# Adding DMAs inside SBUF for two of four weight sums and for the inner blocks' sums to the residual, in a two-layer decoder trunk

## The chip, the core and the metric

The kernel runs on one NeuronCore of a Trainium2 chip. The metric is the device time of one execution in microseconds (us); three executions of the kernel before gave 1259.92, 1260.09 and 1260.38 us, so the median is 1260.09 us. PE is the matrix engine (PEld its weight loads), DVE the vector engine, ACT the scalar engine, POOL the GpSimd engine, SP the engine that issues most DMAs. PSUM is the memory that PE writes its sums to, SBUF the working memory.

## What is computed

A decoder trunk of two layers on 512 tokens with 1024 channels in float32. Each layer has a mixer (pooling, retention and sparse attention heads, one output projection), a layer norm, a gated feed-forward network (FFN) with a causal convolution of width 3, and a second layer norm. The change touches the FFN alone:

```python
def _conv_ffn(x, w_gate, w_up, conv_w, conv_b, w_down):   # x (512, 1024)
    hg = x @ w_gate                                       # (1024, 2816)
    hp = jnp.pad(hg, ((0, 0), (CONV_WIDTH - 1, 0), (0, 0)))
    hc = conv_b
    for kk in range(CONV_WIDTH):
        hc = hc + hp[:, kk:kk + t] * conv_w[kk]
    return (jax.nn.gelu(hc) * (x @ w_up)) @ w_down        # (2816, 1024)
...
x = _layernorm(DEEPNORM_ALPHA * x + f, ln2_g[l], ln2_b[l])
```

## The kernel before

**Precision.** Every product is made of three matmuls (`mm3`): each operand is split into a part that the matrix engine takes exactly (`hi`, a copy) and the rest (`lo`, a subtraction). A weight that was loaded as float32 into a `raw` tile therefore needs one copy, mostly on ACT, and one subtraction, on DVE or POOL, into a `w` tile before PE can use it.

**Tiling of the FFN.** The 2816 inner channels are 22 channel blocks of 128. The first three (`ff_plain`) are made directly. The other 19 of each layer (`ff_seven`) make gate and up of a channel block together by a scheme of seven instead of eight half-size products; it needs, per channel block, seven weight operands, of which three (`11`, `21`, `22`) are loaded and four (`t1` to `t4`) are sums of loaded ones. `load_seven` makes them: four DMAs of 256 KB fill the raw tiles `b` and `r`; one DVE addition of 128x1024 makes `t13` (`t1` and `t3`), two of 128x512 make the two halves of `t24`; seven `split` calls turn them into `w` tiles. `ff_seven` runs 84 matmuls of 256 columns on them; ACT copies its PSUM sums out several times in between, and PE accumulates further into the same PSUM bank after each copy.

**Down projection.** The 22 channel blocks are grouped as `BLOCKS` = 4, 3, 3, 3, 3, 6. When a group is done, 8 tiles (4 token tiles by 2 halves of 512 channels) of the down projection are made in PSUM from the group's `hT` tiles and added to the residual tiles `y` by `add_down`: DVE, 128x512, one operation each. They are mixed in among the matmuls of the next group's channel blocks.

**Order.** All instructions are recorded and then ordered by a list planner (`Plan.schedule`): it prices each (`price`), takes for each engine the first one that is ready by its model, and so writes one fixed order for each engine. At run time each engine works through its order and waits at an instruction whose inputs or buffer are not there yet; whatever stands behind it on that engine waits too. Buffers are pools of equal slots: 5 for `raw`, 14 for `w`, 29 for everything else of that size (`U`), 8 PSUM banks. An instruction that shares SBUF ports between DVE and POOL is kept from overlapping by the planner (`shares`).

Of the kernel before, what the change touches and what calls it, by code (L numbers as in the profile page):

```python
# [18 lines left out]
P = 128  # L19
# [133 lines left out]
class Plan:  # L153
# [49 lines left out]
    def shares(self, e, m, seen):  # L203

        if e == "vector":
            source = [v for read, v in seen if read and not v.tile.psum and int(np.prod(v.shape[1:])) > 1]
            return len(source) > 1 or (m in ("tensor_scalar", "tensor_copy") and not any(v.tile.psum for _, v in seen))
        return e == "gpsimd" and m != "memset"

    def price(self, op, seen):  # L210
        def size(v):
            return int(np.prod(v.shape[1:]))

        n = max([size(v) for _, v in seen] or [1])
        e, m = op.engine, op.method
        if e == "tensor":
            if m == "transpose":
                return 56 if op.args[2].shape[1] == 64 else 110
            n = size(op.args[2])
            return max(107, n * 0.4537)  # L220
        if e == "scalar":
            extra = sum(isinstance(op.kwargs.get(k), View) for k in ("bias", "scale")) + ("accum_out" in op.kwargs)
            return n * 0.833 + (52 if any(v.tile.psum for _, v in seen) else 95) + 92 * extra
        if e == "vector":
            if m == "reciprocal":
                return 6.3 * n + 70
            scalars = sum(isinstance(a, View) for a in (op.args[2:4] if m == "tensor_scalar" else op.args[2:3]))
            if m in ("tensor_scalar", "tensor_copy") and not any(v.tile.psum for _, v in seen):
                return 0.52 * n + 70 + 58 * scalars
            return 1.04 * n + 70 + 55 * scalars * (m == "scalar_tensor_tensor")  # L230
        if e == "gpsimd":
            if m == "memset":
                return n * 0.9 + 20
            if m == "tensor_copy":
                return n * 3.33 + 120
            if m == "tensor_scalar":
                return n * 1.24 + 120
            if op.args[-1] == OP.pow:
                return n * 165 + 300
            return n * 2.16 + 120  # L240
        byte = n * 4 * max(v.shape[0] for _, v in seen)
        return byte / 330.0

    def schedule(self):
# [35 lines left out]
        def opened(op):  # L280

            out = []
            for t in op.tiles:
                if t.got is None:
                    out.append(t)
                    if t.psum:
                        out += [f for f in t.follow if f.got is None and f not in out]
            return out
# [43 lines left out]
        while left:  # L332
            best = None
            for e in self.ENGINES:
                now = free[e]
                w, r = waiting[e], ready[e]
                while w and w[0][0] <= now:
                    heapq.heappush(r, heapq.heappop(w)[1:])
                cand = None
                skipped = []  # L340
                while r:
                    i = heapq.heappop(r)
                    skipped.append(i)
                    at = placed_at(ops[i[1]])
                    if at is not None and at <= now:
                        cand = (now, *i)
                        break
                    if len(skipped) > LOOK:
                        break
                if cand is None:  # L350

                    opts = []
                    for i in skipped:
                        at = placed_at(ops[i[1]])
                        if at is not None:
                            opts.append((at, *i))
                    for t0, *i in heapq.nsmallest(LOOK, w):
                        at = placed_at(ops[i[1]])
                        if at is not None:
                            opts.append((max(at, t0), *i))  # L360
                    if opts:
                        cand = min(opts)
                for i in skipped:
                    heapq.heappush(r, i)
                if cand is not None and (best is None or cand < best[:3]):
                    best = (*cand, e)
            assert best is not None, "no place for any instruction that is ready"
            start, _, i, e = best
            op = ops[i]
            if (op.rank, i) in ready[e]:  # L370
                ready[e].remove((op.rank, i))
                heapq.heapify(ready[e])
            else:
                waiting[e] = [x for x in waiting[e] if x[2] != i]
                heapq.heapify(waiting[e])
            op.start = start
            end = start + op.cost
            if e == "scalar" and op.method == "activation":
                f = op.args[2]
                if any(f in s for s in FUNCTIONS) and f not in functions:  # L380
                    functions = next(s for s in FUNCTIONS if f in s)
                    end += 1290
            if op.shared:
                held[e == "vector"] = end
            free[e] = end
            if e == "sync":
                free[e] = start + 60
                dma = max(getattr(self, "dma", 0.0), start + 600)
                self.dma = dma + op.cost
                end = self.dma + 1500  # L390
            elif e == "gpsimd":
                free[e] = end + 100
            op.opens = opened(op)
            op.wait = -1
            for t in op.opens:
                place = min(slots[t.key])
                slots[t.key].remove(place)
                t.got, t.after = place[0], place[2]
                if t.psum:
                    used[t.psum] += 1  # L400
            for t in op.tiles:
                t.last, t.by = max(t.last, end), e
                t.left -= 1
                if t.left == 0:
                    slots[t.key].append((t.last + 200, next(number), t))
                    if t.psum:
                        used[t.psum] -= 1
            for u in op.users:
                u.wait -= 1
                u.ready = max(u.ready, end + LATENCY[e][u.engine] * SLACK["wait"])  # L410
                if u.wait == 0:
                    heapq.heappush(waiting[u.engine], (u.ready, u.rank, u.index))
            done.append(op)
            left -= 1
# [12 lines left out]
def trunk(tc, x_d, pos_d, w_in, w_out, w_gate, w_up, w_down, cst_d, prm_d,  # L427
# [4 lines left out]
    with es:  # L432
# [84 lines left out]
        def load_seven(l, f):  # L517

            wg, wu = (w[l].rearrange("(h k p) c -> p h k c", p=P, h=2)[:, :, :, f * P:(f + 1) * P] for w in (w_gate, w_up))
            b, r = raw_tile(2, 4, P), raw_tile(2, 4, P)  # L520
            for out, src in ((b[:, 0], wg[:, 0]), (r[:, 0], wu[:, 0]), (b[:, 1], wu[:, 1]), (r[:, 1], wg[:, 1])):
                nc.sync.dma_start(out, src)
            t13, t24 = raw_tile(2, 4, P), raw_tile(2, 4, P)
            out = {}

            def split(name, src):
                w = w_tile(2, 4, P)
                nc.scalar.copy(w[:, 0], src)
                engine("v" if f >= NFF - 2 else SEVEN[name]).tensor_tensor(w[:, 1], src, w[:, 0].bitcast(F), OP.subtract)
                out[name] = (w[:, 0], w[:, 1])  # L530

            split("11", b[:, 0])
            nc.vector.tensor_tensor(t13, b, r[:, 0:1].to_broadcast([P, 2, 4, P]), OP.add)
            split("t1", t13[:, 0])
            split("21", r[:, 1])
            nc.vector.tensor_tensor(t24[:, 0], t13[:, 0], b[:, 1], OP.add)
            split("t2", t24[:, 0])
            split("22", b[:, 1])
            nc.vector.tensor_tensor(t24[:, 1], t24[:, 0], r[:, 1], OP.add)
            split("t3", t13[:, 1])  # L540
            split("t4", t24[:, 1])
            return out
# [335 lines left out]
        for l in range(L):  # L878
# [640 lines left out]
            def add_down(q, ib, t, lo, hi):  # L1519

                y = y_t[t][:, lo:hi]
                if ib == 0:
                    nc.vector.scalar_tensor_tensor(y, y, ALPHA, q, OP.mult, OP.subtract)
                else:
                    nc.vector.tensor_tensor(y, y, q, OP.subtract)

            xT2 = None
            wd = [None, None]
# [184 lines left out]
```

## Time and profile before

| | |
|---|---|
| median of 3 executions | 1260.09 us |
| profiled execution: its time, its span | 1259.87 us, 1258.1 us |
| granted TensorE clock, mean | 0.999 of 2.4 GHz |
| busy share PE, PEld | 98%, 89% |
| busy share DVE, ACT, POOL | 82%, 56%, 27% |
| chain of work that ended last: PE, DVE | 92%, 5% |
| DMA: mean rate, share of the 16 DMA engines in the load queue | 98 GB/s, 32% |

The span runs from the first to the last instruction; the profiled time has 1.8 us around it. Most operations are recorded through one helper, so that they all carry its line, L424; groups of the profile are told apart by their tiles. The busy time of PE overlaps from one matmul to the next, so that the pitch (start to start) is what a matmul costs, not its own duration.

### The profile page before, as it was taken

The numbers are of one execution on the slowest core, as the hardware profiler recorded it, in microseconds if no ns is written. First come the engines' busy times: TensorE is split into PE (matmuls) and PEld (weight loads), VectorE is DVE, ScalarE is ACT, GpSimd is POOL, SyncE is SP. The second block draws the span as 40 slices with busy tenths as digits, with TensorE's granted clock in tenths as the row PEclk, the third lists the DMA queues.
The fourth block names the chain that finished last, engine by engine and source line by source line (L and its number), as shares of the span: only waits on it lengthen the run. The fifth ranks groups of instructions, "written<-read, shape, count | busy, mean of one in ns | idle before, by whom it ended". The sixth has DMA issues, their size and how long they took to land.

```text
span 1258.1 us, 21371 instructions
## 1 busy us (share of the span) xinstructions
PE 1238.4 (98%) x8004; PEld 1120.6 (89%) x8004; DVE 1030.6 (82%) x1915; ACT 704.3 (56%) x1458; POOL 336.8 (27%) x247
## 2 busy tenths in 40 slices
PE   8999999999999999999999999999999999999997
PEld 6789898889998999999877898888899999999996
DVE  7868888788698988888877688888787889888876
ACT  6455578675545555556334455876764555555550
POOL 1133212352322322212111422133523222222023
PEclk9999999999999999999999999999999999999999
DMA  8321532102424333345253125221023333334221
GB/s 276 108 79 47 189 101 78 41 2 56 130 76 119 102 93 110 110 129 155 94 162 93 51 68 184 69 84 34 18 80 89 93 102 108 114 96 143 86 84 68
DMA packets 142600, 123.23 MB, mean 98 GB/s; under 512 B 6688, under 2 KB 116000, under 8 KB 142496
## 3 DMA queue, kind: packets, MB, share of 16 engines
q1 hardware_dynamic: 142496, 121.86, 32.0%
q8 instruction: 63, 1.03, 0.3%
q14 instruction: 41, 0.34, 0.1%
HBM read 117.65 MB, written 4.19 MB: 97 GB/s over the span
## 4 chain that ended last, share of the span: by engine, by line
PE 92%; DVE 5%; ACT 1%; issue 1%; SPq 0%; DMA 0%; POOL 0%; POOLq 0%; DVEq 0%; ACTq 0%
PE mm L424 46%; PE s L424 38%; PE tr L424 4%; PE pv L424 3%; DVE y L424 1%; DVE w L424 1%; DVE PT L424 1%; SPq L424 0%; DVE xq L424 0%; DMA raw<-in_w_up 0%; DVE VR L424 0%; DVE sm L424 0%; DVE rt L424 0%; ACT xq L424 0%; ACT xf L424 0%
## 5 line engine op out<-in xcount | busy, mean ns | idle before, releaser
L424 POOL TENSOR_TENSOR w<-raw,w 128x1024 fp32r<-128x1024 f32 (+3 forms) x116 | 234.2, 2020 | 636.4 <-ACT w L424 348.3
L424 ACT CAST w<-raw 128x512 fp32r<-128x512 f32 (+2 forms) x403 | 291.0, 742 | 196.8 <-PE s L424 117.9
L424 DVE TENSOR_TENSOR w<-raw,w 128x512 fp32r<-128x512 f32 (+3 forms) x288 | 236.0, 838 | 40.6 <-ACT w L424 36.1
L424 PE MATMUL mm<-w,hT 128*128 128x512 f32 (+1 forms) x1074 | 262.1, 391 | 1.7 <-ACT hT L424 1.7
L424 PE MATMUL s<-xq,w 128*128 128x256 f32 x1944 | 250.1, 281 | 0.1
L424 PEld LDWEIGHTS s<-xq,w 128*128 128x128 f32 x1944 | 242.4, 188 | 6.4 <-DVE sm L424 0.5
L424 PE MATMUL mm<-w,xT 128*128 128x512 f32 (+3 forms) x1152 | 240.7, 353 | 2.1 <-DVE w L424 1.8
L424 PE MATMUL s<-xs,w 128*128 128x256 f32 x1824 | 233.3, 280 | 0.0
L424 PEld LDWEIGHTS mm<-w,hT 128*128 128x128 f32 x1074 | 193.4, 188 | 39.5 <-ACT hT L424 1.9
L424 PEld LDWEIGHTS s<-xs,w 128*128 128x128 f32 x1824 | 225.3, 189 | 2.2
L424 PEld LDWEIGHTS mm<-w,xT 128*128 128x128 f32 x1152 | 191.0, 188 | 26.7 <-ACT xT L424 2.0
L424 DVE TENSOR_TENSOR raw<-raw,raw 128x512 f32<-128x512 f32 (+1 forms) x114 | 100.7, 883 | 6.0 <-DMA raw<-in_w_up 4.6
L424 DVE TENSOR_TENSOR y<-y,mm 128x512 f32<-128x512 f32 (+1 forms) x97 | 63.3, 674 | 19.8 <-PE mm L424 19.3
L424 ACT COPY pq<-s 128x256 f32<-128x256 f32 x152 | 55.1, 369 | 41.9 <-PE s L424 41.6
L424 PE MATMUL mm<-w,mixT 128*128 128x512 f32 x240 | 73.8, 414 | 0.0
L424 DVE SCALAR_TENSOR_TENSOR pq<-gu,prm,pq 128x511 f32<-128x511 f32 x76 | 67.1, 882 | 4.8 <-ACT pq L424 4.5
L424 POOL TENSOR_TENSOR sm<-sm,mhalf 128x1 f32<-128x1 f32 (+1 forms) x22 | 26.5, 1203 | 124.1 <-DVE sm L424 117.6
L424 DVE TENSOR_TENSOR gu<-s,pq 128x256 f32<-128x256 f32 x76 | 30.8, 419 | 27.7 <-PE s L424 23.7
L424 ACT ACTIVATE P<-s,sm 128x128 f32<-128x128 f32 (+3 forms) x96 | 49.4, 536 | 6.3 <-DVE sm L424 6.2
L424 DVE TENSOR_REDUCE sm<-s 128x1 f32<-128x384 f32 (+4 forms) x88 | 43.1, 528 | 8.6 <-PE s L424 7.9
L424 PEld LDWEIGHTS mm<-w,mixT 128*128 128x128 f32 x240 | 42.5, 189 | 7.0 <-ACT P L424 0.2
L424 PE MATMUL pv<-PT,VS 128*128 128x384 f32 x160 | 48.0, 364 | 0.7 <-ACT P L424 0.4
(203 smaller groups left out, 1654.8 us busy)
## 6 DMA issues: line engine op xcount, KB each, us to landing
raw<-in_w_gate SPq DMA_DIRECT2D x76, 256.0 KB, 3.4
raw<-in_w_up SPq DMA_DIRECT2D x76, 256.0 KB, 3.5
raw<-in_w_down SPq DMA_DIRECT2D x36, 512.0 KB, 3.9
raw<-in_w_in SPq DMA_DIRECT2D x32, 512.0 KB, 4.0
raw<-in_w_out SPq DMA_DIRECT2D x14, 512.0 KB, 3.8
raw<-in_w_in SPq DMA_DIRECT2D x8, 530.0 KB, 3.9
raw<-in_w_down SPq DMA_DIRECT2D x16, 256.0 KB, 2.8
raw<-in_w_in SPq DMA_DIRECT2D x8, 384.0 KB, 3.3
```

The source lines that it names most:

```text
L424: getattr(getattr(self.nc, op.engine), op.method)(*a, **k)
```

## The change

In `load_seven` the tile `r` is gone: the first half of `w_up` is loaded twice, straight into both halves of `t13`, and the fourth quarter of the weights straight into the second half of `t24`. The sum `t13 += b` (128x1024, 512 KB) is no longer a DVE addition but a DMA issued by POOL that adds into its target. In `add_down` the groups 1 to 4 no longer add on DVE: ACT copies the negated PSUM sum into a new `U` tile `yd`, and a DMA issued by POOL adds that tile (256 KB) to `y`. The first and the last group stay on DVE. The planner learns a price (900, times its slack of 1.2) and a latency (4500 ns) for such a DMA, and doesn't count it as sharing ports with DVE.

```diff
-        return e == "gpsimd" and m != "memset"
+        return e == "gpsimd" and m not in ("memset", "dma_start")
...
+            if m == "dma_start":
+                return 900
...
                 free[e] = end + 100
+                if op.method == "dma_start":
+                    end += 4500
...
-            b, r = raw_tile(2, 4, P), raw_tile(2, 4, P)
-            for out, src in ((b[:, 0], wg[:, 0]), (r[:, 0], wu[:, 0]), (b[:, 1], wu[:, 1]), (r[:, 1], wg[:, 1])):
+            b, t13, t24 = (raw_tile(2, 4, P) for _ in range(3))
+            for out, src in ((b[:, 0], wg[:, 0]), (t13[:, 0], wu[:, 0]), (b[:, 1], wu[:, 1]), (t13[:, 1], wu[:, 0]), (t24[:, 1], wg[:, 1])):
                 nc.sync.dma_start(out, src)
-            t13, t24 = raw_tile(2, 4, P), raw_tile(2, 4, P)
+            nc.gpsimd.dma_start(t13, b, accum_op=OP.add)
...
             split("11", b[:, 0])
-            nc.vector.tensor_tensor(t13, b, r[:, 0:1].to_broadcast([P, 2, 4, P]), OP.add)
             split("t1", t13[:, 0])
-            split("21", r[:, 1])
+            split("21", t24[:, 1])
...
-            nc.vector.tensor_tensor(t24[:, 1], t24[:, 0], r[:, 1], OP.add)
+            nc.vector.tensor_tensor(t24[:, 1], t24[:, 0], t24[:, 1], OP.add)
...
                     nc.vector.scalar_tensor_tensor(y, y, ALPHA, q, OP.mult, OP.subtract)
+                elif ib == len(BLOCKS) - 1:
+                    nc.vector.tensor_tensor(y, y, q, OP.subtract)
                 else:
-                    nc.vector.tensor_tensor(y, y, q, OP.subtract)
+                    tmp = U([P, 512], n="yd")
+                    nc.scalar.activation(tmp, q, AF.Copy, scale=-1.0)
+                    nc.gpsimd.dma_start(y, tmp, accum_op=OP.add)
```

## Rows read from the trace of the kernel before

**Rows 1.** The page, part 1: busy time, share and instructions of each engine.
```profile
PE 1238.4 (98%) x8004; PEld 1120.6 (89%) x8004; DVE 1030.6 (82%) x1915; ACT 704.3 (56%) x1458; POOL 336.8 (27%) x247
```

**Rows 2.** Busy time by stretch: the FFN of layer 0 (three), of layer 1 (three).
```profile
core 0: us, PE busy (x) PEld busy (x) DVE busy (x) ACT busy (x) POOL busy (x), PEclk, DMA share, GB/s
290.00:400.00 110.00, 107.48 (x790) 101.58 (x790) 89.61 (x122) 60.63 (x110) 27.50 (x15) 1.00 0.33 94
400.00:600.00 200.00, 200.00 (x1425) 187.62 (x1424) 172.75 (x250) 116.30 (x218) 47.39 (x26) 1.00 0.40 117
600.00:660.00 60.00, 59.56 (x278) 48.22 (x277) 49.97 (x96) 17.70 (x32) 11.18 (x7) 1.00 0.40 125
913.00:1030.00 117.00, 116.22 (x856) 110.10 (x855) 97.53 (x136) 66.38 (x120) 29.60 (x16) 1.00 0.32 95
1030.00:1200.00 170.00, 170.00 (x1209) 159.35 (x1209) 147.69 (x214) 96.26 (x185) 37.85 (x22) 1.00 0.36 106
1200.00:1250.00 50.00, 49.87 (x295) 43.81 (x293) 36.45 (x60) 16.16 (x27) 16.55 (x12) 1.00 0.21 74
```

**Rows 3.** Busy PE, 400 to 600 us, tile s alone, then tile mm alone.
```profile
400.00:600.00 200.00, 140.70 (x1142) 1.00 0.40 117
...
400.00:600.00 200.00, 71.47 (x283) 1.00 0.40 117
```

**Rows 4.** Chain that ended last, 400 to 480 us: start, duration, what.
```profile
442.30 7.12 PE s L424 x60
...
454.15 2.32 PE mm L424 x10
```

**Rows 5.** Groups of instructions (busy, mean ns | idle before); DVE, then ACT.
```profile
L424 DVE TENSOR_TENSOR y<-y,mm 128x512 f32<-128x512 f32 x95 | 62.4, 679 | 17.8 <-PE mm L424 17.4
...
L424 DVE TENSOR_TENSOR raw<-raw,raw 128x1024 f32<-128x1024 f32 x38 | 48.8, 1284 | 4.6 <-DMA raw<-in_w_up 4.6
...
L424 ACT COPY xf<-tr 128x512 f32<-128x512 f32 x16 | 9.6, 601 | 0.0
```

**Rows 6.** Groups, 400 to 600 us: the same two of DVE, POOL's longest.
```profile
L424 POOL TENSOR_TENSOR w<-raw,w 128x1024 fp32r<-128x1024 f32 x9 | 23.4, 2599 | 77.0 <-ACT w L424 37.2 <-PE s L424 32.0 <-ACT gu L424 7.7
L424 DVE TENSOR_TENSOR y<-y,mm 128x512 f32<-128x512 f32 x32 | 20.8, 679 | 2.4 <-PE mm L424 2.2
...
L424 DVE TENSOR_TENSOR raw<-raw,raw 128x1024 f32<-128x1024 f32 x12 | 15.8, 1316 | 0.9 <-DMA raw<-in_w_up 0.9
```

**Rows 7.** Timeline (start, duration in us): one channel block's load, sum, cast, use.
```profile
430.35 0.37 SPq L424 DMA_DIRECT2D raw<-in_w_gate  x1
...
437.98 1.21 DVE L424 TENSOR_TENSOR raw<-raw,raw 128x1024 f32<-128x1024 f32 x1
...
445.21 0.62 ACT L424 CAST w<-raw 128x512 fp32r<-128x512 f32 x1 [1.06 <-PE s L424]
...
457.72 1.58 PE L424 MATMUL s<-xs,w 128*128 128x256 f32 x12
```

**Rows 8.** Timeline: the cast of the next channel block's first sum.
```profile
455.79 1.15 ACT L424 CAST w<-raw 128x512 fp32r<-128x512 f32 x2 [0.38 <-DVE raw L424]
```

**Rows 9.** Timeline, 388 to 397 us: DVE waits for a load, PE idles.
```profile
392.26 1.23 DVE L424 TENSOR_TENSOR raw<-raw,raw 128x1024 f32<-128x1024 f32 x1 [2.89 <-DMA raw<-in_w_up]
...
395.88 1.44 PE L424 MATMUL mm<-w,hT 128*128 128x512 f32 x5 [1.72 <-ACT hT L424]
```

**Rows 10.** Waits of DVE over the span: total, times, longest.
```profile
DVE raw L424 <- DMA raw<-in_w_up: 4.6, 3, 2.9
```

**Rows 11.** DMA, 400 to 600 us; then issues of the span: KB, us to landing.
```profile
DMA packets 29848, 23.39 MB, mean 117 GB/s; under 512 B 1120, under 2 KB 24672, under 8 KB 29830
...
raw<-in_w_down SPq DMA_DIRECT2D x12, 512.0 KB, 4.0
...
xs<-y SPq DMA_DIRECT2D x4, 512.0 KB, 2.9
...
y<-xs SPq DMA_DIRECT2D x4, 512.0 KB, 7.2
```

## The prediction

> **What bounds the kernel now.** I read the engines' shares first: PE is busy for 98% of the span, DVE for 82%, ACT for 56%, POOL for 27% [rows 1]. A busy PE need not be a full one, so I went on to the FFN by stretches [rows 2]. In the middle of each layer's FFN, 400 to 600 us and 1030 to 1200 us, PE is busy for 200.00 of 200 and 170.00 of 170 us, at a granted clock of 1.00. The pitch tells whether that is real work. The chain shows 60 matmuls of 256 columns in 7.12 us, 0.1187 us each, and 10 of 512 columns in 2.32 us, 0.232 us each [rows 4]. In 400 to 600 us there are 1142 of the first and 283 of the second kind [rows 3]: 1142 x 0.1187 + 283 x 0.232 = 135.6 + 65.7 = 201 us, for 200 us of time. PE runs matmul after matmul at its own pitch there, and nothing that DVE does is waited for. DVE is busy for 172.75 of these 200 us, ACT for 116.30, POOL for 47.39 [rows 2]: DVE is close to full and still isn't the bound.
>
> What PE loses in the FFN is the rest of these stretches: 2.52 us in the first, 0.44 in the third, 0.78 in the fourth and 0.13 in the last, 3.9 us in all [rows 2]. One piece of it I can follow: DVE waited 2.89 us for a load before a sum of weights, what stood behind that sum came late, and PE idled for 1.72 us [rows 9]. Everything outside these stretches belongs to mixer, norms and the end, which the change doesn't touch.
>
> **What goes.** 38 sums of 128x1024 leave DVE, 48.8 us together [rows 5], and 4 groups x 8 tiles x 2 layers = 64 additions to the residual at 679 ns, 43.5 us [rows 5]. In 400 to 600 us that is 15.8 + 20.8 = 36.6 us [rows 6], so DVE falls from 172.75 to 136 us of 200. On the path this is worth 0, because PE is full there without it. The cover needs no work to hide it: the removed work was itself hidden. At most it gives back the 3.9 us of PE's losses.
>
> **What comes on ACT.** 64 copies of a 128x512 PSUM tile. The nearest row is ACT's copy of such a tile at 601 ns [rows 5]: 64 x 0.6 = 38.5 us, 19 us of them in 400 to 600 us, so ACT rises from 116 to 136 us of 200. That stays under PE's 200 and costs 0 as a sum. It stands, though, on the engine whose copies PE waits for within a channel block; one of these copies can be late by the 0.6 us that another takes. From PE's side a wait of 2.89 us cost 1.72 us, and the other two of the three DMA waits, 4.6 - 2.9 = 1.7 us together, cost nothing that shows [rows 9, 10]. So I take 0 for a delay of 0.6 us, with 64 x 0.6 = 38 us as an end that would need every copy on the path.
>
> **What comes on POOL.** 102 DMA issues. The trace has no DMA issued by POOL. The nearest rows are SP's issue at 0.37 us [rows 7] and POOL's own longest operation in the stretch at 2.6 us [rows 6]; between them 38 to 265 us on an engine that is idle for about three quarters of the FFN. In 400 to 600 us there are 12 + 32 = 44 issues: at 1 us POOL goes from 47 to 91 us, at 2.6 us to 162 of 200. It costs 0 in either case as a sum. Behind a waiting issue stand POOL's subtractions for `21` and for the down weights, and behind these SP's loads, which need their raw slots.
>
> **What comes on the DMA engines.** Each channel block loads `wu`'s first half once more (256 KB), adds 512 KB inside SBUF, and the residual 64 times 256 KB. In 400 to 600 us that is 12 x 0.26 = 3.1 MB of loads and 12 x 0.52 + 32 x 0.26 = 14.7 MB of additions on top of 23.39 MB, which took a share of 0.40 [rows 2, 11]. If a byte that is added costs what a loaded one does, the share becomes 0.40 x 41.2/23.4 = 0.70; if it costs double, because the target is read too, 0.40 x 55.9/23.4 = 0.96. I take a value between, some 0.8: the added rows are 2 and 4 KB long, and most packets of the loads are under 2 KB [rows 11].
>
> **Where the new waits stand.** The trace has no adding DMA, so its latency is bounded: a transfer of 512 KB out of SBUF lands in 2.9 us, the slowest group of 512 KB transfers into it in 7.2 us [rows 11]. The planner reckons 0.9 x 1.2 + 4.5 = 5.6 us. I take 5.6 us, near the middle, and let 3 to 9 us be the ends. Now the slack. In the row of one channel block the load was issued at 430.35, the sum ran at 437.98, the cast of `t1` at 445.21, after waiting for PE to free a `w` slot, and PE used it at 457.72 [rows 7]. From sum to cast there are 7 us, from cast to use 12.5 us. The next block has less: its cast waited 0.38 us for the sum [rows 8]. But the change needs three raw slots per channel block where there were four (`b`, `r`, `t13`, `t24`), so of five slots two, not one, are free for the next block's `b` and `t13`, and the adding DMA can start before the previous block's casts are done, up to one block's PE time (84 x 0.1187 = 10 us) earlier. That hides 5.6 us, and mostly 9 us. The additions to `y` are needed one group later, some 40 us; only their `yd` slot is held. The term is 0, with an end of 38 x 1.72 = 65 us if each adding DMA cost PE what the one late load did [rows 9].
>
> **Sum.** 1259.87 (profiled; the median is 0.2 us above) - 0 to 3.9 + 0 = 1256 to 1260; I take **1260.0 us**, since the one traceable loss hangs on a load, and loads get more company.
>
> **The rivals.**
>
> **The weight sums come late** (slower). An ACT cast or DVE sum behind an adding DMA waits at the head of its engine, and PE's PSUM copies stand behind it. This decides from a latency beyond what the planner reckoned plus about 1 to 3 us: three DMA waits show that 1.7 us in two cost nothing and 2.9 us cost 1.72 us [rows 9, 10]. With a quarter of 38 sums so late: 9.5 x 1.72 = 16 us, 1276 us. With all: 1325 us. For it speak the load bursts that such a DMA shares the engines with and the fixed order; against it the 7 + 12.5 us of slack [rows 7]. The Trainium skill has a rule that would bring this about: "SBUF — State Buffer", summary of rules for kernel authors, says that a DMA issued by GpSimd is starved of descriptor writing while DVE runs in its two-port fast modes. The stretch's large DVE groups that I read are two-operand additions [rows 6], which that page does not count among these modes, so I give the rule no more than a part of this chance.
>
> **DVE's relief reaches PE** (faster). All 3.9 us of PE's losses go: 1259.9 - 3.9 = 1256.0 us. For it: the one loss that I can follow runs through DVE [rows 9]. Against: its cause was a load, not DVE's work, and the rest is fractions of a microsecond.
>
> **The DMA engines become the bound** (much slower). If an added byte costs three times a loaded one, the share in 400 to 600 us is 0.40 x 70.6/23.4 = 1.2, and the FFN's 707 us [rows 2] grow by up to 20%, 140 us; at a share of 1.05 by 35 us, 1295 us. The Trainium skill, "DMA: Bandwidth & Descriptors", section on issuing engines not being separate DMA queues, says that DMAs of SP, ACT and GpSimd share the same 16 engines; no run here shows it for GpSimd yet.
>
> That the change doesn't do what it says, in that the work still falls on DVE, is ruled out by the edit; that it buys nothing is my forecast.
>
> **How the numbers follow.** Forecast (within the FFN's slack) 0.53; sums late 0.27; DMA engines the bound 0.08; relief reaches PE 0.12. What a measurement here can tell from no change is about 0.2%, 2.5 us. The likeliest case alone is 1257.5 to 1262.5 us. The range of 8 in 10 takes in the relief (1256) and the first half of the late sums (1276). Faster 0.12, same 0.53, slower 0.35.
>
> **What would show it.** In the profile after: DVE's busy time down by about 92 us, ACT's up by about 38 us, PE still at 200 of 200 in the middle of the FFN, no wait for the adding DMA over 2 us on ACT or DVE, DMA share in the FFN's middle about 0.7 to 0.95. I am wrong if PE idles before a matmul that waits for an ACT copy behind a wait for `t13` or a `yd` slot, or if loads land several us later than now.

## The result and the profile after

The changed kernel took 1280.26 us (median of four executions, 1279.74 to 1280.77) against 1260.10 us before it: ratio 1.0155, 95% interval 1.0143 to 1.0167. It is 20 us slower, outside the range of 1256 to 1276 us. The profiled execution has a span of 1278.0 us, 19.9 us more than before.

The page of the changed kernel, part 1 and the DMA queues of part 3 (packets, MB, share of 16 engines); these lines answer to [rows 1]:

```profile
PE 1246.0 (97%) x8004; PEld 1124.6 (88%) x8004; DVE 963.8 (75%) x1813; ACT 736.8 (58%) x1522; POOL 419.9 (33%) x349
...
q1 hardware_dynamic: 162560, 131.83, 34.0%
q0 software_dynamic: 14688, 36.71, 16.4%
```

The work moved as intended: DVE lost 66.8 us of busy time, ACT gained 32.5 us, POOL 83.1 us. The cost appears at PE: span less busy time was 19.7 us and is 32.0 us, so 12.3 of the 19.9 us are PE's idle time. Of the other 7.6 us some 3.8 us are the clock: the mean granted clock fell from 0.999 to 0.996, 0.004 x 1278 - 0.001 x 1258 = 3.8 us, an estimate from rounded means. The last 3.8 us lie in gaps too short to show between overlapping matmuls, or elsewhere; I could not assign them.

Busy time by stretch of the changed kernel, columns as in [rows 2]:

```profile
290.00:400.00 110.00, 109.74 (x810) 104.25 (x811) 82.88 (x117) 64.61 (x114) 33.93 (x23) 1.00 0.55 141
400.00:500.00 100.00, 98.43 (x682) 90.90 (x681) 70.49 (x101) 62.80 (x124) 45.43 (x38) 1.00 0.84 195
500.00:600.00 100.00, 93.53 (x675) 87.83 (x674) 66.48 (x99) 58.05 (x112) 26.86 (x24) 0.98 0.79 193
...
1030.00:1130.00 100.00, 99.80 (x699) 92.66 (x699) 73.46 (x98) 63.00 (x122) 43.94 (x38) 1.00 0.84 195
1130.00:1200.00 70.00, 65.01 (x462) 60.98 (x460) 47.51 (x69) 42.28 (x84) 25.21 (x22) 0.98 0.84 194
1200.00:1250.00 50.00, 48.05 (x311) 43.39 (x312) 31.64 (x45) 25.07 (x45) 11.58 (x8) 1.00 0.45 114
```

Start at PE's column. The first stretch is better than before, 109.74 of 110 us instead of 107.48 [rows 2]. The next loses 1.6 us. Only the last group of channel blocks is bad: 6.5 us are lost in 500 to 600 us, 5.0 us in 1130 to 1200 us and 2.0 us in 1200 to 1250 us. The DMA share, 0.32 to 0.40 before over the same stretches up to 1200 us [rows 2], is 0.55 in the first stretch and 0.79 to 0.84 from 400 to 600 and from 1030 to 1200 us.

The waits of the changed kernel (total, times, longest) name the path; before, only the first line has a counterpart, DVE's 4.6 us for a load [rows 10]:

```profile
DVE raw L428 <- DMA raw<-raw: 45.7, 18, 6.2
ACT w L428 <- DMA raw<-raw: 34.0, 18, 4.1
PE s L428 <- ACT pq L428: 13.6, 10, 3.2
ACT hT L428 <- DMA y<-yd: 2.6, 2, 1.9
```

DVE and ACT wait 36 times for the adding DMAs of the weight sums (`raw<-raw`), and PE waits for ACT's copies of PSUM sums (`pq`), which need no DMA. How the one becomes the other is seen in one place, in the timeline of the changed kernel (start, duration, what, idle before and its releaser):

```profile
520.53 1.73 SPq L428 DMA_DIRECT2D raw<-in_w_up  x2
...
528.13 0.88 POOL L428 DMA_DIRECT2D raw<-raw  x1 [5.07 <-DMA raw<-in_w_up]
...
535.43 1.66 ACT L428 CAST w<-raw 128x512 fp32r<-128x512 f32 x3 [3.38 <-DMA raw<-raw]
535.43 0.69 DVE L428 TENSOR_TENSOR raw<-raw,raw 128x512 f32<-128x512 f32 x1 [5.71 <-DMA raw<-raw]
...
538.22 0.63 ACT L428 COPY pq<-s 128x256 f32<-128x256 f32 x2
...
538.63 4.61 PE L428 MATMUL s<-xs,w 128*128 128x256 f32 x24 [2.53 <-ACT pq L428]
```

The load is issued at 520.5, and POOL can issue the sum only at 528.1, when the last of the loads is there. The sum lands 7.3 us later. ACT and DVE have stood at the head of their queues for 3.4 and 5.7 us; ACT must now make three casts, an activation and a fourth cast before it reaches the copy that PE wants, and PE idles for 2.5 us. The clock follows, in stretches of 10 us of PE alone (PE busy, granted clock, DMA share, GB/s):

```profile
530.00:540.00 10.00, 7.47 (x59) 0.99 0.57 122
540.00:550.00 10.00, 10.00 (x60) 0.84 0.52 145
```

After the stretch in which PE was busy for 7.47 us of 10, the granted clock of the next is 0.84, a mean of the levels 2.4 and 1.2 GHz; 10 x 0.16 = 1.6 us more are gone.

### The profile page after: what moved, and what is told of

Its sections match the earlier page's. It is cut to its first block, busy times and chain, and to the rows that moved or that the text cites. A ratio compares the mean times of both kernels' runs of the same rounds, so it can differ in the third digit from the quotient of the medians.

```text
span 1278.0 us, 21809 instructions
## 1 busy us (share of the span) xinstructions
PE 1246.0 (97%) x8004; PEld 1124.6 (88%) x8004; DVE 963.8 (75%) x1813; ACT 736.8 (58%) x1522; POOL 419.9 (33%) x349
## 3 DMA queue, kind: packets, MB, share of 16 engines
q1 hardware_dynamic: 162560, 131.83, 34.0%
q0 software_dynamic: 14688, 36.71, 16.4%
## 4 chain that ended last, share of the span: by engine, by line
PE 80%; DMA 8%; DVE 6%; issue 3%; ACT 2%; POOL 1%; SPq 1%; POOLq 0%; ACTq 0%; DVEq 0%
PE mm L428 42%; PE s L428 30%; PE tr L428 5%; PE pv L428 3%; DMA raw<-raw 3%; DMA raw<-in_w_up 2%; DVE w L428 2%; DMA raw<-in_w_gate 1%; DMA y<-yd 1%; DVE y L428 1%; ACT w L428 1%; DVE PT L428 1%; SPq L428 1%; DVE raw L428 0%; POOL y L428 0%
## 5 line engine op out<-in xcount | busy, mean ns | idle before, releaser
L428 PE MATMUL s<-xs,w 128*128 128x256 f32 x1824 | 237.2, 284 | 14.8 <-ACT pq L428 13.2
L428 DVE SCALAR_TENSOR_TENSOR pq<-gu,prm,pq 128x511 f32<-128x511 f32 x76 | 61.4, 808 | 34.1 <-ACT pq L428 33.3
L428 POOL DMA_DIRECT2D y<-yd x64 | 58.0, 925 | 85.9 <-ACT yd L428 73.7
L428 DVE TENSOR_TENSOR raw<-raw,raw 128x512 f32<-128x512 f32 x38 | 30.6, 805 | 45.8 <-DMA raw<-raw 45.7
L428 DVE TENSOR_TENSOR hT<-pq,hT 128x512 fp32r<-128x512 f32 x38 | 50.6, 1332 | 18.6 <-ACT hT L428 18.5
L428 POOL TENSOR_TENSOR sm<-sm,mhalf 128x1 f32<-128x1 f32 (+1 forms) x22 | 27.5, 1250 | 107.7 <-DVE sm L428 101.2
L428 POOL DMA_DIRECT2D raw<-raw x38 | 34.4, 905 | 74.5 <-DMA raw<-in_w_up 38.7
L428 POOL TENSOR_SCALAR P<-P,sm 128x384 f32<-128x384 f32 (+3 forms) x40 | 22.2, 569 | 86.2 <-DVE sm L428 72.8
```

The costliest lines, as they stand in the source:

```text
L428: getattr(getattr(self.nc, op.engine), op.method)(*a, **k)
```

## The experiments

Every run stands beside the kernel before on the same chip (1260.3 to 1261.7 us); ratios are to it.

**One half of the change at a time.** `weights_only` keeps the diff in `load_seven` and puts `add_down` back:

```diff
-                elif ib == len(BLOCKS) - 1:
-                    nc.vector.tensor_tensor(y, y, q, OP.subtract)
                 else:
-                    tmp = U([P, 512], n="yd")
-                    nc.scalar.activation(tmp, q, AF.Copy, scale=-1.0)
-                    nc.gpsimd.dma_start(y, tmp, accum_op=OP.add)
+                    nc.vector.tensor_tensor(y, y, q, OP.subtract)
```

> Only the weight sums are made by adding DMAs (38 of 512 KB, and the first half of w_up loaded twice); all sums to the residual stay on DVE. Changed kernel 1280.3 us, before 1260.1 us. Theory 'late weight sums' (ACT and DVE stand at the head of their queues for the 512 KB adding DMA, which lands later than the 5.6 us that the order reckons): the cause is all here, 1272 to 1281 us. Theory 'crowded DMA engines' (share 0.82 in the FFN's middle, so that loads and adding DMAs are late together): a third to a half of the slowdown is left, 1264 to 1270 us, and the adding DMAs land 1 us or more earlier than the 5.9 us median. Theory 'held yd slots and ACT's extra copies': 1260 to 1262 us.

Measured: 1259.11 us, ratio 0.9986 (0.9977 to 0.9996). `residual_only` keeps the diff in `add_down` and puts `load_seven` back.

> Only the inner groups' sums to the residual are made by adding DMAs (64 of 256 KB, each after a copy on ACT); the weight sums are as before the change. 'Late weight sums': 1259 to 1262 us. 'Crowded DMA engines': 1262 to 1268 us. 'Held yd slots and ACT's extra copies': 1272 to 1281 us.

Measured: 1266.88 us, ratio 1.0047 (1.0032 to 1.0062). The halves cost -1.9 and +5.9 us, the whole +20: some 16 us arise only from the two together. None of the three theories fits both runs: the one that lets the weight sums alone cost nothing puts the whole slowdown on the sums to the residual. The waits for the weight sums in `weights_only`:

```profile
ACT w L428 <- DMA raw<-raw: 13.7, 12, 3.1
DVE raw L428 <- DMA raw<-raw: 12.8, 12, 2.8
PE s L428 <- ACT pq L428: 0.4, 1, 0.4
```

24 waits of up to 3.1 us, 26.5 us in all, cost PE 0.4 us. Waits of that size are covered; those of the changed kernel, up to 6.2 us, are not.

**Another reckoned latency.** `plan_8us`:

```diff
-                    end += 4500
+                    end += 8000
```

> The changed kernel, but the planner reckons 8000 ns instead of 4500 ns for an adding DMA, so that what needs its result is put later in the order; the work is the same. 'Late weight sums': what stood behind the wait now stands ahead of it; most of the slowdown goes, 1261 to 1268 us. 'Crowded DMA engines': the DMAs stay as slow and PE still runs out of weights, 1275 to 1285 us.

Measured: 1267.14 us, ratio 1.0050 (1.0033 to 1.0067). The same work in another order gives two thirds of the slowdown back, as the late sums want it. The waits that were 45.7 and 34.0 us, in this run:

```profile
ACT w L428 <- DMA raw<-raw: 5.5, 2, 3.8
DVE raw L428 <- DMA raw<-raw: 4.7, 3, 2.2
```

**Half as many bytes to add.** `half_weight_add`:

```diff
-            nc.gpsimd.dma_start(t13, b, accum_op=OP.add)
+            nc.gpsimd.dma_start(t13[:, :, 0:2], b[:, :, 0:2], accum_op=OP.add)
```

> The changed kernel in the same order on every engine, but each adding DMA of the weight sums adds only half of its elements (256 instead of 512 KB); the other half of the two sums is left out of the computation. 'Late weight sums': the DMA lands 1 to 2 us earlier, inside what the order reckons, and most of the slowdown goes: 1261 to 1268 us. 'The order itself is worse' (ACT's extra copies, the slots): 1277 to 1281 us. 'Crowded DMA engines': in between, 1268 to 1274 us.

Measured: 1281.89 us, ratio 1.0163 (1.0145 to 1.0180). This speaks against the late sums. Its queue and issues:

```profile
q0 software_dynamic: 19552, 26.75, 12.8%
...
L428 POOL DMA_DIRECT2D raw<-raw x38 | 47.1, 1240 | 64.5 <-DMA raw<-in_w_up 32.0
```

With 10 MB less there are 19552 instead of 14688 packets, because each row is now two pieces of 1 KB instead of one of 4 KB; POOL's issue takes 1240 ns instead of 905. The run changed two things at once and decides nothing about the bytes. It leaves an open end: its weight sums land in 4.8 us in the median instead of 5.9, and ACT and DVE wait 18.4 and 30.0 us for them instead of 34.0 and 45.7, yet PE's waits for `pq` grew from 13.6 to 17.1 us. What made up for the earlier landing (POOL's issues grew) was not tested. The next three runs shorten the DMAs without more pieces.

**Duration taken away in the unchanged order.** Only at the point where the planned instructions are issued, each adding DMA is cut to one short piece of each row (64 KB in all); every engine's order stays that of the changed kernel, and the rest of the sums is left out. The edit of `tiny_both`; `tiny_residual` and `tiny_weights` keep one of the cases:

```diff
+            if op.engine == "gpsimd" and op.method == "dma_start":
+                weights = len(op.args[0].shape) == 4
+                if weights:
+                    a = [v[:, 0, 0] for v in a]
+                if not weights:
+                    a = [v[:, 0:128] for v in a]
```

> The changed kernel in its own order on every engine, all 102 adding DMAs kept, but each adds only 128 elements of a row (64 KB instead of 512 and 256 KB); the rest of these sums is left out. Theory 'adding DMAs land late and crowd the loads': with almost nothing to move they land in 2 to 3 us and the time falls to 1258 to 1263 us. Theory 'the written order and POOL's queue' (ACT's copies stand ahead of weight casts, issues wait behind issues): stays at 1272 to 1281 us.

> The same, but only the 64 sums to the residual are cut to 64 KB; the weight sums add their full 512 KB. 'Late through crowding, both streams': 1262 to 1270 us. 'Late weight sums alone': 1272 to 1280 us. 'Order and POOL's queue': 1272 to 1281 us.

> The same, but only the 38 weight sums are cut to 64 KB; the sums to the residual add their full 256 KB. 'Late through crowding, both streams': 1262 to 1270 us. 'Late weight sums alone': 1258 to 1264 us, and then the run with halved weight sums stayed slow only because its halves, two pieces in a row, doubled the descriptors. 'Order and POOL's queue': 1272 to 1281 us.

| weight sums | sums to the residual | time, us | ratio to before |
|---|---|---|---|
| 512 KB | 256 KB | 1280.3 | 1.0155 (1.0143 to 1.0167) |
| 512 KB | 64 KB | 1265.9 | 1.0046 (1.0031 to 1.0061) |
| 64 KB | 256 KB | 1257.7 | 0.9978 (0.9969 to 0.9988) |
| 64 KB | 64 KB | 1257.7 | 0.9980 (0.9971 to 0.9990) |

In this order the written sequence, ACT's 64 extra copies, POOL's queue and the `yd` slots cost nothing by themselves: with short DMAs the kernel is 2.6 us faster than before. The sums to the residual cost nothing either, as long as the weight sums land at once. So all of the slowdown needs the full weight sums: they cost 8 us by themselves, and another 14 us together with the full sums to the residual. `tiny_residual` came out as the theory of crowding by both streams had it, `tiny_weights`, within 0.3 us, as that of late weight sums alone; neither theory foresaw the four times together.

Two things go with the cut that these runs do not separate from the shorter duration. A short weight sum touches only the first piece of a row and waits for the loads of that piece alone: in `tiny_both` the issue at 522.60 us was released by a load that landed at 521.9 us, ahead of the block's last load of `w_up`, which landed at 522.9 us; in the changed kernel the issue at 528.13 us stood behind the later of the two. And a short sum to the residual gives its `yd` slot back earlier: in the changed kernel ACT's `hT` and DVE's `gu` waited 4.0 us in all for `y<-yd` to land (in `tiny_residual` 0.4 us), once with 0.36 us of idle PE soon after it.

From issue to landing, 500 to 600 us, POOL's DMAs on raw tiles (min, median, max), first the changed kernel:

```profile
DMA to landing us min/median/max: 5.8/7.3/7.8
```

then `tiny_residual`:

```profile
DMA to landing us min/median/max: 5.6/5.9/7.7
```

then `tiny_both`:

```profile
DMA to landing us min/median/max: 2.4/4.2/4.7
```

The planner had reckoned 5.6 us. In layer 1, 1130 to 1200 us, the medians of the changed kernel and of `tiny_residual` lie together, 6.1 and 6.3 us (longest 8.4 and 8.0); there the loads of `w_up` differ, 4.7 against 4.2 us. In the earlier groups, 300 to 500 us, the changed kernel's sums land after 4.6 to 6.8 us, median 5.5, and PE loses little.

**What stays with 8000 ns.** `plan_8us_tiny` is that order with all adding DMAs cut in the same way; `weights_8us` is `weights_only` with 8000 ns.

> The order of the run with 8000 ns reckoned (1267.1 us), all adding DMAs cut to 64 KB, the rest of these sums left out. If what is left there, 6 us, still comes from DMAs that land late: 1257 to 1260 us. If this order itself starves PE (raw tiles held longer, loads issued later): 1264 to 1267 us.

> Only the weight sums by adding DMAs (1259.1 us with 4500 ns reckoned), now with 8000 ns reckoned for each. If what little is lost there still comes from sums that land after the reckoned time (12 waits of ACT and 12 of DVE, up to 3.1 us): 1257 to 1258.5 us. If a later place in the order costs raw slots instead: 1260 to 1264 us.

Measured: 1260.56 us, ratio 0.9995 (0.9986 to 1.0004), and 1259.47 us, ratio 0.9986 (0.9977 to 0.9995). Both times lie just outside the ranges given. Most of the 6 us left in `plan_8us` go with the adding DMAs' length; beside the 1257.7 us of the short DMAs this order itself is 3 us worse. For the weight sums alone, which land near the reckoned time (5.3 us in the median), a larger reckoning changes nothing.

**More buffers.** `six_raw`, and three runs beside it:

```diff
-NU, NW, NR = 29, 14, 5
+NU, NW, NR = 28, 14, 6
-NS = 16
+NS = 14
```

> The changed kernel with six instead of five raw slots (28 instead of 29 general slots, 14 instead of 16 small ones), the same work. 'Late weight sums': with a further slot the loads and so the sums of the last group's channel blocks start earlier, 1262 to 1272 us. If only the reckoned latency matters: 1276 to 1284 us.

> Only the weight sums by adding DMAs, with six raw slots (28 general, 14 small). 'Late weight sums': no worse than 1259.1 us and down to 1257.5 us, the level of the kernels whose sums land at once. If one general slot less costs more: 1261 to 1270 us.

Measured: 1290.39 us, ratio 1.0227 (1.0211 to 1.0242), and 1261.55 us, ratio 1.0004 (0.9994 to 1.0013). The first was outside what either theory gave. The sixth raw slot took the place of one general slot, and a kernel that now needs `yd` tiles can miss it. `six_raw_tiny` has the short DMAs, `five_raw_28` 28 general slots and five raw ones.

> The order of the run with six raw slots (1290.4 us), all 102 adding DMAs cut to 64 KB, the rest of these sums left out. 'Late adding DMAs': the whole slowdown goes, 1257 to 1262 us. 'One general slot less, so that yd tiles hold up others': 1275 us or more stay.

> The changed kernel with one general slot less (28) and 14 small ones, five raw slots as before. If the further slowing by six raw slots came from the missing general slot: 1286 to 1294 us. If it came from what six raw slots let start earlier: 1277 to 1284 us.

Measured: 1282.89 us, ratio 1.0169 (1.0152 to 1.0185), and 1297.23 us, ratio 1.0277 (1.0251 to 1.0302). The first is in the range of the missing general slot, the second above both of its ranges. So with 28 general slots and 14 small ones the full change costs 17 us more than with 29 and 16, and with six raw slots most of the slowdown stays when the DMAs are short. At 28, the sixth raw slot brings 7 us, in the direction that late sums want. The waits of PE in `six_raw_tiny`, none of which stands in `tiny_both`:

```profile
PE s L431 <- ACT pq L431: 10.5, 10, 1.6
PE s L431 <- ACT w L431: 3.3, 2, 1.7
```

Nothing waits for a weight sum there. ACT stands at casts that wait for PE, with the copies that PE wants behind them; in one place (start, duration, what, idle before and its releaser):

```profile
567.83 0.62 ACT L431 CAST w<-raw 128x512 fp32r<-128x512 f32 x1 [1.42 <-PE s L431]
568.36 0.64 ACT L431 COPY pq<-s 128x256 f32<-128x256 f32 x2
568.78 1.44 PE L431 MATMUL s<-xs,w 128*128 128x256 f32 x10 [1.02 <-ACT pq L431]
```

So this part points to the order that the planner writes with these slots. Which of them bring it about, the general one or the two small ones, is not shown.

**The 6 us of the sums to the residual alone.** `res_only_tiny` cuts their DMAs to 64 KB, `res_only_short` ACT's 64 copies too (128 of 512 columns).

> The kernel with sums to the residual alone (1266.9 us) in its own order, each of its 64 adding DMAs cut to 64 KB, the rest of these sums left out. If its 6 us come from late adding DMAs or the loads that they delay: 1259 to 1262 us. If they come from ACT's 64 extra copies ahead of the copies that PE waits for, or from the yd slots' place in the order: 1265 to 1267 us.

> The kernel with sums to the residual alone, in its own order, with both ACT's 64 copies and the adding DMAs cut to 128 of 512 columns, the rest of these sums left out. If its 6 us come from the time of ACT's copies: 1260 to 1262 us. If they come from the order that the planner wrote, whatever the copies cost: 1264 to 1267 us.

Measured: 1265.83 us, ratio 1.0046 (1.0031 to 1.0061), and 1264.94 us, ratio 1.0029 (1.0018 to 1.0039). The DMAs are not it. Short copies give perhaps a third back, with intervals that overlap; what is left stays when DMAs and copies are both short, and so goes with the order that the planner wrote for this kernel. Two waits of PE in `residual_only`:

```profile
PE mm L428 <- ACT hT L428: 3.0, 2, 2.0
PE s L428 <- ACT pq L428: 2.2, 5, 0.7
```

Before, PE waited for `hT` once, 1.72 us [rows 9], and not for `pq`, so these waits account for 3.5 of the 5.9 us. Why the planner's order is worse with the new copies in it is not shown.

**A better version.** `weights_only` is the fastest kernel here that computes everything (`weights_8us` has the same ratio): 0.14% below before, with an interval that excludes 1 and an effect below the 0.2% that the prediction counts as a change.

## Why the prediction was wrong

**Right: the bound, and the ceiling of the gain.** PE was full without the removed work. With the adding DMAs all but free the kernel gains 2.6 us, within the 0 to 3.9 us that the prediction took from PE's losses [rows 2]; the loss that it could follow [rows 9] is gone in the changed kernel too.

**Right: the small terms.** ACT's copies were put at 601 ns [rows 5]; the 64 measure 596 ns. POOL's issues were bounded by 0.37 and 2.6 us; they measure about 0.9 us. These groups of the changed kernel (busy, mean ns | idle before):

```profile
L428 ACT ACTIVATE yd<-mm 128x512 f32<-128x512 f32 x64 | 38.1, 596 | 12.5 <-PE mm L428 11.4 <-DVE pq L428 0.7
...
L428 POOL DMA_DIRECT2D raw<-raw x38 | 34.4, 905 | 74.5 <-DMA raw<-in_w_up 38.7 <-DVE pq L428 15.8 <-DVE w L428 8.6
```

The DMA share was put at some 0.8 and is 0.79 to 0.84. An adding byte costs (16.4/36.71) / (34.0/131.83) = 1.7 loaded ones, between the one and two of the working. DVE's busy time fell by 67 us, not 92: its 38 subtractions into `hT` grew from 836 to 1332 ns, 31.8 to 50.6 us in all. The rest of the difference I did not follow.

**Wrong: the term of the new waits.** "That hides 5.6 us, and mostly 9 us ... The term is 0." It is 22.6 us (1280.3 less 1257.7, the time with short weight sums). The trace shows the sign that the prediction named for being wrong: PE idles before a matmul that waits for an ACT copy behind a wait for `t13`. Two steps of the term failed.

First, the slack was read from one channel block in the middle of the FFN [rows 7] and applied to all 38. In 400 to 500 us ACT and DVE already wait 8 times for a sum, up to 3.5 us, and PE loses 1.6 us; in the last group the waits grow to 5.7 us in layer 0 and 6.2 us in layer 1. The chain of the changed kernel there runs through the load and the sum one after the other (start, duration):

```profile
518.86 1.65 POOL w L428
...
520.94 6.51 DMA raw<-in_w_up
...
528.13 7.28 DMA raw<-raw
...
540.71 4.88 DMA raw<-in_w_up
...
572.48 7.82 DMA raw<-raw
```

From 520.94 us to the landing of the sum at 535.41 us pass 14.5 us, and a channel block's matmuls take PE 10 us. The raw slots that I took for free were no help: the load could start only when POOL's subtraction had read the slot. Why the last group is worse than the middle is argued, not shown: less of the down projection is mixed in there, 33 matmuls of 512 columns in 550 to 600 us where before had 67.

Second, the latency of each DMA was bounded by itself, though the share of the engines was worked out in the paragraph ahead of it. The loads of `w_up` have a median of 4.1 us where they had 3.5 over the kernel, and 5.8 us where they had 4.0 in 500 to 600 us (4.3 in `tiny_residual`); the weight sums take 5.9 us over the kernel and 7.3 us in 500 to 600 us, where the 5.6 us of the planner stood. In stretches of 10 us the engines are full, columns as above (the share is of summed packet times and can pass 1):

```profile
520.00:530.00 10.00, 10.00 (x79) 9.65 (x78) 8.33 (x14) 6.25 (x13) 3.52 (x4) 1.00 0.95 216
550.00:560.00 10.00, 9.95 (x78) 9.30 (x76) 5.94 (x11) 5.72 (x13) 3.75 (x4) 1.00 1.09 254
1150.00:1160.00 10.00, 10.00 (x80) 9.70 (x80) 8.88 (x11) 7.39 (x15) 5.04 (x5) 1.00 1.00 191
```

From 500 to 600 us four stretches of 10 us have 0.95 or more; in `tiny_residual` one has, 0.97, and before none has more than 0.72. At the end of the third of these stretches, at 1159.2 us, the sum was issued that took 8.4 us. The 64 sums to the residual, costed at nothing because they are needed a group later, cost 14 us by being in the others' way, perhaps in part through their `yd` slots, which no run separates. The Trainium skill, "DMA: Bandwidth & Descriptors", section on issuing engines not being separate DMA queues, states that DMAs of SP, ACT and GpSimd run on the same 16 engines and interleave. The trace agrees: with POOL's sums to the residual cut, SP's loads of `w_up` in 500 to 600 us fall from 5.8 to 4.3 us and the weight sums from 7.3 to 5.9 us.

**The rivals.** "The weight sums come late" is what happened, at 0.27, and it ended 4 us above the 1276 us at which the range cut it. Its price was put per event, 1.72 us for a wait of 2.89 us. That was too steep for one wait: 24 waits up to 3.1 us cost 0.4 us in `weights_only`. And a quarter of the sums was too few: ACT and DVE each waited for 18 of 38. "The DMA engines become the bound" had the right resource and the wrong form: they are full for stretches of 10 us and answer late there, but over the last group, with a share of 0.79 to 0.84, PE is still busy for 93% of the time. The Trainium skill's rule on starved descriptor writing ("SBUF — State Buffer", summary of rules) is not needed for this, and no run here tests it: POOL's issues take 0.9 us in the changed kernel as in `tiny_both`, and DVE works beside them in both.

## What to carry to other kernels

Where an engine works through a fixed order, a DMA in place of an operation is priced by its latency at the crowding that the change itself creates, against the shortest slack among all its places, not the slack of a typical one. Transfers that hardly anybody waits for still delay those that somebody does. And to tell a transfer's duration from the order in which it stands, shorten the transfer and keep the order; mind that its pieces don't become more, and that it still waits for the same inputs.

## What the runs showed of the hardware

An adding DMA of 512 KB inside SBUF took 4.4 us at the least from issue to landing (`weights_8us`) and 9.2 us at the most (`six_raw`); one of 64 KB 2.3 us at the least, 3.5 us in the median (`tiny_both`, weight sums). The Trainium skill's fit for a DMA from GpSimd ("DMA: Bandwidth & Descriptors", section on the anatomy of one DMA on that path) gives an estimate of 2.0 + 0.524/0.436 = 3.2 us for 512 KB and 2.15 us for 64 KB: the small one agrees with the least that was measured, the large one doesn't, and here the measurement decides.

That two changes which cost -2 and +6 us alone cost 20 us together, with an order written afresh for each, I had not expected; nor that one general slot of 29 and two small ones of 16 could cost 17 us.
